# The second sparse tile of an expert layer: half of its value rows weighed and added on VectorE instead of by matmuls

## The chip, the cores and the metric

One core of a Trainium2 chip runs the whole kernel in one launch. The metric is the device time of that launch in microseconds (us), lower is better. TensorE is called PE here, its weight loads PEld, VectorE DVE, ScalarE ACT, GpSimd POOL and SyncE SP.

## The reference, cut to what matters

One layer over 512 latent tokens of width 1024: attention, and then a retrieval of single-neuron experts. The attention part is untouched by the change. The retrieval is this:

```python
def one(xc):                                   # a chunk of 128 tokens
    ...
    ids = ...                                  # (128, 8, 16): 16 experts for each of 8 heads
    g = jax.nn.softmax(best, axis=-1)
    ue = jnp.take(u, ids, axis=0)              # u, v: (16384, 1024) float32
    ve = jnp.take(v, ids, axis=0)
    a = jax.nn.gelu(jnp.einsum('cd,chkd->chk', xc, ue), approximate=False)
    return jnp.einsum('chk,chkd->cd', (g * a).astype(xc.dtype), ve)
```

So each token has 128 slots (8 heads times 16), each slot an expert number and a weight, and a token's output is the sum over its 128 slots of weight times a row of 1024 values of the table v.

## The kernel before, in words

The 512 tokens are four tiles of 128. Tiles 1 and 2 are **dense**: a loop of 128 steps (line 1218) reads the whole tables u and v, 128 rows a step, and works with matmuls whose operands are split in a high and a low part of a narrower float format, so that one product is three matmuls (`mm3`, lines 93 to 96). In each step, and in two halves `b` of it, `split_u` and `split_v` split what was loaded (ACT makes the high part at line 90, DVE the low part at line 91: tiles `uhi`, `ulo`, `vhi`, `vlo`), `scores_u` multiplies tokens with u into `pa`, `weigh` (line 1187) makes the weights from `pa` (gelu on ACT, line 1193; times the gates on DVE, line 1194; high part on ACT, low part on DVE: `ga`, `wdhi`, `wdlo`), and `add_v` adds the weighted rows of v into `accd`.

Tiles 0 and 3 (`FIRST`, `LAST`) are **sparse**: only the rows that a token needs are fetched, by gathers on POOL (`gather`, line 425). One gather brings 128 rows of 4 KB, 512 KB in all, into one of nine buffers that are used in turn (`gbuf`). `sparse_u` takes the 128 slots one by one: a gather brings for each of the 128 tokens its row of u, and one DVE instruction (line 917) multiplies and sums it. `sparse_v` (line 934) then turns weights and expert numbers around by two transposes, so that a gather (`idT`) brings all 128 slots of one token. A group of four gathers, of tokens that lie 32 apart, is used by matmuls (line 957): the weights stand in a masked tile `wm` of 32 columns, of which only that token's is not zero, so the four tokens' matmuls lie in four column strips of PE. After 32 groups `acc` holds the tile's output, and `finish` (line 927) scales it, adds the residual, normalizes and stores.

The gathers are pulled from a generator (`sparse`, line 1167) inside the dense loop, at a pace that spreads what is left evenly over its steps (lines 1243 to 1245). A gather's use is not written at once but put off (`later`, `settle`, lines 876 to 903): a use on DVE until five more gathers have been issued (`LAG2`), a group of four for PE until eight have. The gathers of tile 0's v and tile 3's u are mixed until about 1480 us; from there on all gathers are tile 3's v. Until about 1620 us the dense loop also builds gates for its last quarter (`gates`, lines 1102 to 1113, on DVE, PE and ACT). A scheduler then lays the instructions out engine by engine; each engine runs its own in the order that it has them.

Loads of u and v for the dense loop go through SP's queue (lines 1028 and 1033), 512 KB each, with three buffers for u and two for v.

Of the kernel before, what the change touches and what calls it, by code (L numbers as in the profile page):

```python
# [12 lines left out]
F32 = mybir.dt.float32  # L13
F32R = mybir.dt.float32r
BF16 = mybir.dt.bfloat16
I32 = mybir.dt.int32
U32 = mybir.dt.uint32
AF = mybir.ActivationFunctionType
OP = mybir.AluOpType
# [3 lines left out]
P = 128  # L23
D = 1024
# [14 lines left out]
SLOTS = PH * TOPK  # L39
NEG = -3.0e38  # L40
SB = 16
FIRST, DENSE, LAST = 0, (1, 2), 3
# [19 lines left out]
def tile_layer(ctx: ExitStack, tc: tile.TileContext, aps):  # L62
    nc = tc.nc
# [3 lines left out]
    ident = cst.tile([P, P], F32, name="ident")  # L67
# [64 lines left out]
    for t in range(NKT):  # L132
        xt[t] = xp.tile([P, D], F32, name=f"x{t}")
        src = aps["ctx"][0, t * P : (t + 1) * P, :] if t < NCT else aps["x"][0, (t - NCT) * P : (t - NCT + 1) * P, :]
        (nc.scalar if t % 2 else nc.sync).dma_start(xt[t], src)

    pt = ps0.tile([P, 80], F32, name="pt", tag="t")
# [249 lines left out]
    keep = ctx.enter_context(tc.tile_pool(name="keep", bufs=1, side="right"))  # L387
    rows_ = {}
# [23 lines left out]
    idis = {t: keep.tile([P, SLOTS], I32, name=f"idi{t}") for t in SPARSE}  # L412
    idfs = {t: keep.tile([P, SLOTS], F32, name=f"idf{t}") for t in SPARSE}
    gs = {t: keep.tile([P, TOPK, PH], F32, name=f"g{t}") for t in SPARSE}
    seld = {}
    u_tab = aps["peer_u"][0]
    v_tab = aps["peer_v"][0]
# [3 lines left out]
    def gather(tab, col):  # L421
        pool, tag, n = gbufs["all"][gbufs["n"] % len(gbufs["all"])]
        gbufs["n"] += 1
        b_ = (gp if pool == "gp" else pool).tile([P, D], F32, name="gbuf", tag=tag, bufs=n)
        nc.gpsimd.indirect_dma_start(  # L425
            out=b_, out_offset=None, in_=tab, in_offset=bass.IndirectOffsetOnAxis(ap=col, axis=0)
        )
        return b_
# [141 lines left out]
    def norm_row(pool, src, a_row, dst, add_row=None):  # L570
        s_ = pool.tile([P, 1], F32, name="nss", tag="nss")
        nc.scalar.activation(dst, src, AF.Square, accum_out=s_)
        r_ = pool.tile([P, 1], F32, name="nrs", tag="nrs")
        rsqrt_mean(r_, s_, D)
        nc.vector.scalar_tensor_tensor(dst, src, r_, a_row, op0=OP.mult, op1=OP.mult)
        if add_row is not None:
            nc.vector.tensor_tensor(dst, dst, add_row, op=OP.add)
# [293 lines left out]
    acts = {}  # L871
# [4 lines left out]
    def later(use, several=False):  # L876

        pending.append((gbufs["n"], several, use))
        settle()

    def settle(all_of=None):
        while pending:
            n, several, use = pending[0]
            if all_of is None:
                out = gbufs["n"] - n
                full = out + 1 >= len(gbufs["all"])
                if not several and out < lag[0]:
                    return
                if several and not full and (out < lag[0] + GROUP - 1 or sum(p[1] for p in pending) < GROUP):
                    return  # L890
            elif all_of not in [p[2] for p in pending]:
                return
            if not several:
                pending.pop(0)
                use(0)
                use(1)
                continue
            group = [p for p in pending if p[1]][:GROUP]
            for p in group:
                pending.remove(p)  # L900
            for b in range(2):
                for p in group:
                    p[2](b)

    def flush(use):
        settle(use)

    def sparse_u(t):
        a = gp.tile([P, SLOTS], F32, name="a", tag="a", bufs=2)
        acts[t] = a  # L910
        for k in range(SLOTS):
            ub = gather(u_tab, idis[t][:, k : k + 1])

            def use(b, ub=ub, k=k):
                if b:
                    return
                tc.keep_in_program_order(nc.vector.scalar_tensor_tensor(ub, ub, 1.0, h2s[t], op0=OP.mult, op1=OP.mult, accum_out=a[:, k : k + 1]))  # L917

            later(use)
            yield  # L920
        flush(use)

    def load_x1(t, x1):
        nc.sync.dma_start(x1, out[0, t * P : (t + 1) * P, :])
        return x1

    def finish(t, acc, x1):
        o = gp.tile([P, D], F32, name="o", tag="gbuf", bufs=GBUFS)
        nc.vector.tensor_tensor(o, acc.rearrange("p b n -> p (b n)"), rows_["g2"], op=OP.mult)
        nc.vector.tensor_tensor(x1, x1, o, op=OP.add)  # L930
        norm_row(fp, x1, rows_["fg"], o)
        nc.sync.dma_start(out[0, t * P : (t + 1) * P, :], o)

    def sparse_v(t):
        a = acts[t]
        nc.scalar.activation(a, a, AF.Gelu)
        nc.vector.tensor_tensor(a, a, gs[t].rearrange("p k h -> p (k h)"), op=OP.mult)
        pt = psV.tile([P, 2, 512], F32, name="ptw", tag="acc")
        nc.tensor.transpose(pt[:, 0, :P], a, ident)
        nc.tensor.transpose(pt[:, 1, :P], idfs[t], ident)  # L940
        wT = vp.tile([P, 4, 32], F32, name="wT", tag="wT")
        nc.vector.tensor_copy(wT.rearrange("p c r -> p (c r)"), pt[:, 0, :P])
        idT = vp.tile([P, P], I32, name="idT", tag="idT")
        nc.vector.tensor_copy(idT, pt[:, 1, :P])
        acc = psV.tile([P, 2, 512], F32, name="acc", tag="acc")
        for r in range(32):
            if r % 4 == 0:
                wm = vp.tile([P, 4, 4, 32], F32, name="wm", tag="wm", bufs=2)
                nc.vector.tensor_tensor(
                    wm, eye32[:, r : r + 4].unsqueeze(1).to_broadcast([P, 4, 4, 32]),  # L950
                    wT[:, :, r : r + 4].unsqueeze(3).to_broadcast([P, 4, 4, 32]), op=OP.mult,
                )
            for c in range(4):
                vb = gather(v_tab, idT[:, 32 * c + r : 32 * c + r + 1])

                def use(b, vb=vb, w=wm, c=c, r=r):
                    tc.keep_in_program_order(nc.tensor.matmul(  # L957
                        acc[32 * c : 32 * c + 32, b, :], w[:, c, r % 4], vb[:, 512 * b : 512 * b + 512],
                        start=(r == 0), stop=(r == 31), skip_group_check=True,
                    ))  # L960

                later(use, True)
                yield
        x1 = load_x1(t, keep.tile([P, D], F32, name="x1f", tag="a2"))
        flush(use)
        while "fg" not in rows_:
            yield
        finish(t, acc, x1)

    gp = ctx.enter_context(tc.tile_pool(name="gp", bufs=1, side="right"))  # L970
    slx = ExitStack()
    sl = slx.enter_context(tc.tile_pool(name="sl", bufs=2, side="right"))
    o = [gp.tile([P, KC, P], F32, name="o0", tag="gbuf", bufs=GBUFS)]
# [9 lines left out]
    def early():  # L983
        for _ in first:
            posts[0] += 1
            yield
        posts[0] = NK
        g2 = mod_rows(pp0, psP, "a", ("g2",))
        for k, _ in enumerate(sparse_u(FIRST)):
            if k in (6, 12, 18):  # L990
                next(g2, None)
            yield
        gbufs["all"].append(("gp", "h2x", 1))
        lag[0] = max(lag[0], LAG1)
        yield from sparse_v(FIRST)
# [3 lines left out]
    o = [gp.tile([P, KC, P], F32, name="oT", tag="ox", bufs=3) for _ in rest]  # L999
# [7 lines left out]
    vp = ctx.enter_context(tc.tile_pool(name="vp", bufs=1, side="right", reuse_waits="tile"))  # L1007
    eye32 = vp.tile([P, 32, 32], BF16, name="eye32")
# [5 lines left out]
    psV = ctx.enter_context(tc.tile_pool(name="psV", bufs=1, space=PSUM, reuse_waits="tile"))  # L1014
# [101 lines left out]
    with ExitStack() as es:  # L1116
# [36 lines left out]
        n = NPRE // 2  # L1153
# [13 lines left out]
    def sparse():  # L1167

        second, n, share = sparse_u(LAST), 0, 0.95 * (2 * SLOTS - gbufs["n"]) / SLOTS
        for _ in second:  # L1170
            yield
            n += share
            while n >= 1:
                n -= 1
                if next(fill, fill) is not fill:
                    yield
        for _ in fill:
            yield
        yield from sparse_v(LAST)

    psB = ctx.enter_context(tc.tile_pool(name="psB", bufs=1, space=PSUM, reuse_waits="tile"))
    psD = ctx.enter_context(tc.tile_pool(name="psD", bufs=1, space=PSUM, reuse_waits="tile"))
    sp = sparse()
    fd = ctx.enter_context(tc.tile_pool(name="fd", bufs=2, reuse_waits="tile"))
    accd = psD.tile([P, len(DENSE), 2, 512], F32, name="accd")

    def weigh(i):
# [30 lines left out]
    for i in range(NK + 2):  # L1218
        q, e = i // QI, i % QI
# [32 lines left out]
    for s in range(len(DENSE)):  # L1252
        finish(DENSE[s], accd[:, s], x1d[s])
# [50 lines left out]
```

## Time and profile before

| | |
|---|---|
| median of 3 runs (lowest, highest) | 1859.14 us (1855.89, 1860.36) |
| the profiled execution: its time / its span | 1860.77 us / 1859.0 us |
| mean granted clock of PE | 0.937 |
| busy: PE, DVE, ACT, POOL | 86%, 70%, 39%, 37% |
| read from memory | 472.88 MB, 257 GB/s over the span |

PE's busy time counts matmuls that overlap, so a busy PE is not PE at its peak. A share over the whole span is a mean of stages with different limits; stages are read in the windows below.

### The profile page before, as it was taken

How to read it: one execution, taken by the hardware profiler on the slowest of the kernel's cores; microseconds unless marked ns; L12 is line 12 of the kernel's file. 1: busy time of each engine (PE TensorE's matmuls, PEld its weight loads, DVE VectorE, ACT ScalarE, POOL GpSimd, SP SyncE). 2: the span in 40 equal slices, each digit the busy share in tenths (PEclk: the TensorE clock that was granted, in tenths of full speed). 3: DMA queues.
4: the chain of work that ended last, by engine and by line, in shares of the span. 5: the costliest groups of instructions: out<-in, count | busy, mean ns of one | idle time of the engine just before them, and what ended most of it. 6: DMA issues, size and time to landing. Idle time of an engine off the chain costs nothing.

```text
span 1859.0 us, 30825 instructions
## 1 busy us (share of the span) xinstructions
PE 1592.6 (86%) x11767; PEld 1225.0 (66%) x11767; DVE 1293.1 (70%) x2923; ACT 732.8 (39%) x1441; POOL 693.0 (37%) x607
## 2 busy tenths in 40 slices
PE   4999898757788577898499899899999989999996
PEld 1778567636563476566266778787778767777774
DVE  3623534687776898998688789798889855555545
ACT  4432554435661232111144444344444433444443
POOL 2212200045554685443424334344344333343431
PEclk9999988976889799999799999899999999999998
DMA  8222633555559885967577898898899798899994
GB/s 298 76 68 68 230 97 122 187 186 172 185 189 324 289 315 217 381 242 255 190 271 261 303 333 301 294 354 303 321 344 354 263 362 280 298 347 357 352 353 168
DMA packets 148085, 479.10 MB, mean 258 GB/s; under 512 B 15889, under 2 KB 16993, under 8 KB 147937
## 3 DMA queue, kind: packets, MB, share of 16 engines
q0 software_dynamic: 73728, 268.47, 40.7%
q1 hardware_dynamic: 73200, 206.96, 31.3%
q8 instruction: 92, 1.51, 0.3%
q10 hardware_dynamic: 1008, 1.70, 0.3%
q14 instruction: 57, 0.46, 0.1%
HBM read 472.88 MB, written 4.19 MB: 257 GB/s over the span
## 4 chain that ended last, share of the span: by engine, by line
PE 37%; DVE 5%; DMA 4%; issue 4%; ACT 1%; POOL 1%; another core or an unknown queue 0%; ACTq 0%; DVEq 0%; POOLq 0%; SPq 0%
PE accd L94 6%; PE accd L96 5%; PE acc L957 5%; PE accd L95 5%; PE pa L94 5%; PE pa L96 5%; PE pa L95 4%; PE pg L1111 3%; DMA vraw<-in_peer_v_dram 2%; DMA gbuf<-in_peer_u_dram,idi 1%; DVE gbuf L917 1%; DVE vlo L91 1%; POOL gbuf L425 1%; DMA gbuf<-in_peer_v_dram,idT 1%; DVE oj L1102 1%
## 5 line engine op out<-in xcount | busy, mean ns | idle before, releaser
L425 POOL DMA_INDIRECT gbuf<-in_peer_v_dram,idT x256 | 275.4, 1076 | 457.6 <-PE acc L957 290.5
L425 POOL DMA_INDIRECT gbuf<-in_peer_u_dram,idi x256 | 314.8, 1230 | 312.1 <-DVE gbuf L917 169.4
L917 DVE SCALAR_TENSOR_TENSOR gbuf<-gbuf,h 128x1024 f32<-128x1024 f32 x256 | 320.7, 1277 | 32.1 <-DMA gbuf<-in_peer_u_dram,idi 31.6
L90 ACT CAST vhi<-vraw 128x512 fp32r<-128x512 f32 x256 | 157.8, 620 | 254.0 <-PE accd L96 196.2
L91 DVE TENSOR_TENSOR vlo<-vraw,vhi 128x512 fp32r<-128x512 f32 x256 | 174.9, 688 | 115.5 <-ACT vhi L90 88.2
L94 PE MATMUL pa<-h2Thi,uhi 128*128 128x256 f32 x848 | 244.6, 288 | 11.1 <-ACT ga L1193 10.2
L95 PE MATMUL pa<-h2Tlo,uhi 128*128 128x256 f32 x848 | 242.9, 286 | 0.6 <-issue 0.6
L96 PE MATMUL pa<-h2Thi,ulo 128*128 128x256 f32 x848 | 242.5, 286 | 0.8 <-issue 0.8
L94 PE MATMUL accd<-vhi,wdhi 128*128 128x512 f32 x512 | 215.4, 421 | 21.1 <-ACT wdhi L90 17.2
L96 PE MATMUL accd<-vhi,wdlo 128*128 128x512 f32 x512 | 207.0, 404 | 6.0 <-DVE wdlo L91 4.8
L95 PE MATMUL accd<-vlo,wdhi 128*128 128x512 f32 x512 | 206.7, 404 | 3.5 <-DVE vlo L91 2.7
L91 DVE TENSOR_TENSOR ulo<-uraw,uhi 128x512 fp32r<-128x512 f32 x212 | 146.6, 692 | 57.7 <-ACT uhi L90 47.8
L90 ACT CAST uhi<-uraw 128x512 fp32r<-128x512 f32 x212 | 131.3, 620 | 129.3 <-PE pa L95 65.4
L94 PEld LDWEIGHTS pa<-h2Thi,uhi 128*128 128x128 f32 x848 | 165.0, 195 | 26.1 <-ACT ga L1193 16.3
L95 PEld LDWEIGHTS pa<-h2Tlo,uhi 128*128 128x128 f32 x848 | 164.9, 194 | 9.1 <-issue 1.1
L96 PEld LDWEIGHTS pa<-h2Thi,ulo 128*128 128x128 f32 x848 | 164.6, 194 | 2.1 <-issue 1.6
L94 PEld LDWEIGHTS accd<-vhi,wdhi 128*128 128x128 f32 x512 | 98.6, 193 | 76.7 <-issue 38.9
L957 PE MATMUL acc<-gbuf,wm 128*32 128x512 f32 x1024 | 143.7, 618 | 0.9 <-DMA gbuf<-in_peer_v_dram,idT 0.6
L1102 DVE TENSOR_TENSOR oj<-iota,ijT 128x2048 bf16<-128x2048 bf16 x64 | 79.9, 1248 | 76.8 <-PE accd L96 24.2
L1111 PE MATMUL pg<-og,oj 128*128 128x32 bf16 x3072 | 101.0, 177 | 34.8 <-DVE og L1107 20.0
L1111 PEld LDWEIGHTS <-oj 128*128 128x128 bf16 x3072 | 88.2, 97 | 56.4 <-issue 26.7
L96 PEld LDWEIGHTS accd<-vhi,wdlo 128*128 128x128 f32 x512 | 98.0, 192 | 34.7 <-DVE wdlo L91 12.2
(278 smaller groups left out, 2855.3 us busy)
## 6 DMA issues: line engine op xcount, KB each, us to landing
uraw<-in_u_turned_dram SPq DMA_DIRECT2D x128, 512.0 KB
vraw<-in_peer_v_dram SPq DMA_DIRECT2D x128, 512.0 KB
wraw<-in_w_mod_dram SPq DMA_DIRECT2D x24, 1024.0 KB
wraw<-in_peer_wq_dram SPq DMA_DIRECT2D x16, 1024.0 KB
wraw<-in_w_in_dram SPq DMA_DIRECT2D x8, 1024.0 KB
wraw<-in_w_out_dram SPq DMA_DIRECT2D x4, 1024.0 KB
wraw<-in_w_out_dram SPq DMA_DIRECT2D x8, 512.0 KB
gbuf<-in_peer_u_dram,idi POOLq DMA_INDIRECT x256
```

The lines of the kernel that those rows point to most:

```text
L90: nc.scalar.copy(hi, src)
L91: (eng or nc.vector).tensor_tensor(lo, src, hi.bitcast(F32), op=OP.subtract)
L94: nc.tensor.matmul(ps, ahi, bhi, start=first, stop=False)
L95: nc.tensor.matmul(ps, ahi, blo, start=False, stop=False)
L96: nc.tensor.matmul(ps, alo, bhi, start=False, stop=last)
L425: nc.gpsimd.indirect_dma_start(out=b_, out_offset=None, in_=tab, in_offset=bass.IndirectOffsetOnAxis(ap=col, axis=0))
L917: tc.keep_in_program_order(nc.vector.scalar_tensor_tensor(ub, ub, 1.0, h2s[t], op0=OP.mult, op1=OP.mult, accum_out=a[:, k : k + 1]))
L957: tc.keep_in_program_order(nc.tensor.matmul(acc[32 * c : 32 * c + 32, b, :], w[:, c, r % 4], vb[:, 512 * b : 512 * b + 512], start=(r == 0 ...
L1102: nc.vector.tensor_tensor(oj, row(iota2, NK), over(ijT[t][:, 1, ts], NK), op=OP.is_equal)
L1111: nc.tensor.matmul(pg[:, r], oj[:, r // 2, :, r % 2], og[:, w, r // 2, :, r % 2], start=(w == 0), stop=(w == 2))
```

## The change

The second sparse tile (tile 3) gets `sparse_v_halves` in place of `sparse_v`; tile 0 keeps `sparse_v`. Of the 128 slots, the last 64 are still used by matmuls, but a gather now brings two tokens with 64 slots each, so that the 128 tokens take 64 gathers and 16 groups of four. The first 64 slots are gathered slot by slot, as for u: a gather brings for each of the 128 tokens its row of v for one slot, and one DVE instruction multiplies it with the token's weight and adds it to the tile `sums` in SBUF (4 KB in each partition, new). Four gathers of the one kind and four of the other alternate, 128 in all as before. `finish` adds `sums` and `acc` by one more DVE instruction. The tile of masked weights is built in two halves of 64 partitions, and the two transposes read a copy (`twice`) in which the 64 slots stand twice.

```diff
-    def finish(t, acc, x1):
+    def finish(t, acc, x1, more=None):
...
-        nc.vector.tensor_tensor(o, acc.rearrange("p b n -> p (b n)"), rows_["g2"], op=OP.mult)
+        if more is None:
+            nc.vector.tensor_tensor(o, acc.rearrange("p b n -> p (b n)"), rows_["g2"], op=OP.mult)
+        else:
+            nc.vector.tensor_tensor(more, more, acc.rearrange("p b n -> p (b n)"), op=OP.add)
+            nc.vector.tensor_tensor(o, more, rows_["g2"], op=OP.mult)
...
+    HS = SLOTS // 2
+    def sparse_v_halves(t, sums):
...
+        for w, src in enumerate((a, idfs[t])):
+            nc.vector.tensor_copy(tw[:, w], src[:, HS:].unsqueeze(1).to_broadcast([P, 2, HS]))
...
+        for r in range(16):
+            if r % 4 == 0:
+                wm = vp.tile([P, 4, 4, 32], F32, name="wm", tag="wm", bufs=2)
+                for e in range(2):
...
+            for c in range(4):
+                vb = gather(v_tab, idT[:, 16 * c + r : 16 * c + r + 1])
+
+                def use(b, vb=vb, w=wm, c=c, r=r):
+                    tc.keep_in_program_order(nc.tensor.matmul(
+                        acc[32 * c : 32 * c + 32, b, :], w[:, c, r % 4], vb[:, 512 * b : 512 * b + 512],
+                        start=(r == 0), stop=(r == 15), skip_group_check=True,
+                    ))
+
+                later(use, True)
+                yield
+            for k in range(4 * r, 4 * r + 4):
+                vb = gather(v_tab, idis[t][:, k : k + 1])
+
+                def add(b, vb=vb, k=k):
...
+                    if k == 0:
+                        ins = nc.vector.tensor_scalar(sums, vb, a[:, 0:1], None, op0=OP.mult)
+                    else:
+                        ins = nc.vector.scalar_tensor_tensor(sums, vb, a[:, k : k + 1], sums, op0=OP.mult, op1=OP.add)
...
+                later(add)
+                yield
...
-        yield from sparse_v(LAST)
+        yield from sparse_v_halves(LAST, sums)
...
+    sums = ctx.enter_context(tc.tile_pool(name="sums", bufs=1)).tile([P, D], F32, name="sums")
```

On DVE, late in the dense loop (no gates are built there any more), one step and a half stood like this before; `ulo` and `vlo` are the low parts of the loads, `ga` and `wdlo` those of the weights:

```order
L1194 TENSOR_TENSOR ga<-ga,Gb 128x256
L91 TENSOR_TENSOR vlo<-vraw,vhi 128x512
L91 TENSOR_TENSOR wdlo<-ga,wdhi 128x256
L91 TENSOR_TENSOR ulo<-uraw,uhi 128x512
L91 TENSOR_TENSOR vlo<-vraw,vhi 128x512
L91 TENSOR_TENSOR ulo<-uraw,uhi 128x512
L1194 TENSOR_TENSOR ga<-ga,Gb 128x256
```

Now a like place reads as follows (line 1194 is now 1262, and line 1028 is the new addition):

```order
L91 TENSOR_TENSOR wdlo<-ga,wdhi 128x256
L1028 SCALAR_TENSOR_TENSOR sums<-gbuf,a,sums 128x1024
L91 TENSOR_TENSOR ulo<-uraw,uhi 128x512
L1028 SCALAR_TENSOR_TENSOR sums<-gbuf,a,sums 128x1024
L91 TENSOR_TENSOR vlo<-vraw,vhi 128x512
L1028 SCALAR_TENSOR_TENSOR sums<-gbuf,a,sums 128x1024
L1262 TENSOR_TENSOR ga<-ga,Gb 128x256
L91 TENSOR_TENSOR ulo<-uraw,uhi 128x512
```

Three of a block's four additions stand in one step, one of them directly ahead of `ga`; the fourth comes a step later, and a third step has none.

On POOL, the order of the gathers from where tile 3's u ends was this before:

```order
L425 DMA gbuf<-in_peer_u_dram,idi_1502 128x1024 x2
L425 DMA gbuf<-in_peer_v_dram,idT 128x1024 x2
L425 DMA gbuf<-in_peer_u_dram,idi_1502 128x1024 x4
L425 DMA gbuf<-in_peer_v_dram,idT 128x1024 x132
L1299 UNCONDITIONAL_BRANCH
```

Now the gathers for PE (`idT`) and for DVE (`idi`) alternate by fours from the same place on:

```order
L425 DMA gbuf<-in_peer_u_dram,idi_1502 128x1024 x4
L425 DMA gbuf<-in_peer_v_dram,idT 128x1024 x8
L425 DMA gbuf<-in_peer_v_dram,idi_1502 128x1024 x4
L425 DMA gbuf<-in_peer_v_dram,idT 128x1024 x4
L425 DMA gbuf<-in_peer_v_dram,idi_1502 128x1024 x4
```

Their number is the same; which engine gives a buffer back is what differs.

At the end of the kernel DVE's order now is this, where before `o<-acc` came directly behind the last `wdlo`:

```order
L1028 SCALAR_TENSOR_TENSOR sums<-gbuf,a,sums 128x1024
L91 TENSOR_TENSOR wdlo<-ga,wdhi 128x256
L1028 SCALAR_TENSOR_TENSOR sums<-gbuf,a,sums 128x1024 x2
L932 TENSOR_TENSOR sums<-sums,acc 128x1024
L933 TENSOR_TENSOR o<-sums,g_3192 128x1024
```

The last additions and one more instruction of 128x1024 stand ahead of the tile's scaling.

## Rows read from the trace of the kernel before

**Rows 1.** The page: engines over the span, and the span in 40 slices.
```profile
PE 1592.6 (86%) x11767; PEld 1225.0 (66%) x11767; DVE 1293.1 (70%) x2923; ACT 732.8 (39%) x1441; POOL 693.0 (37%) x607
...
PE   4999898757788577898499899899999989999996
DVE  3623534687776898998688789798889855555545
...
DMA  8222633555559885967577898898899798899994
```

**Rows 2.** Windows: stretch, PE, PEld, DVE, ACT, POOL busy, clock, DMA share, GB/s.
```profile
1050.00:1450.00 400.00, 376.06 (x3270) 311.24 (x3269) 342.08 (x636) 171.68 (x333) 164.54 (x141) 0.97 0.89 323
1500.00:1620.00 120.00, 113.07 (x1015) 86.87 (x1014) 65.56 (x120) 47.73 (x93) 40.47 (x42) 1.00 0.86 303
1640.00:1800.00 160.00, 160.00 (x1063) 120.96 (x1061) 80.34 (x139) 70.03 (x135) 61.66 (x62) 1.00 0.95 357
```

**Rows 3.** The chain of waits, late: start us, length us, what.
```profile
1644.34 1.85 PE acc L957 x16
...
1818.91 1.85 PE acc L957 x16
1839.73 3.62 PE acc L957 x32
```

**Rows 4.** Groups by line, 1640 to 1800 us: busy, mean ns, idle before.
```profile
L425 POOL DMA_INDIRECT gbuf<-in_peer_v_dram,idT x62 | 62.4, 1006 | 98.6 <-PE acc L957 84.6 <-issue 11.9 <-PE accd L96 1.2
...
L957 PE MATMUL acc<-gbuf,wm 128*32 128x512 f32 x256 | 30.8, 598 | 0.0
```

**Rows 5.** Windows, as in rows 2: the fullest stretches of the DMA engines.
```profile
740.00:790.00 50.00, 41.53 (x208) 26.42 (x207) 44.55 (x246) 6.64 (x14) 23.63 (x23) 0.92 0.99 379
750.00:760.00 10.00, 10.00 (x48) 5.91 (x42) 8.10 (x57) 0.00 (x0) 7.02 (x8) 0.93 1.02 409
1690.00:1700.00 10.00, 10.00 (x68) 7.54 (x68) 4.96 (x10) 4.71 (x9) 3.63 (x4) 1.00 1.00 358
```

**Rows 6.** Groups by line, 1050 to 1450 us (u gathered slot by slot).
```profile
L917 DVE SCALAR_TENSOR_TENSOR gbuf<-gbuf,h 128x1024 f32<-128x1024 f32 x99 | 119.2, 1220 | 6.9 <-DMA gbuf<-in_peer_u_dram,idi 6.9
L94 PE MATMUL pa<-h2Thi,uhi 128*128 128x256 f32 x409 | 118.4, 289 | 6.6 <-ACT ga L1193 6.0 <-issue 0.5
...
L94 PE MATMUL accd<-vhi,wdhi 128*128 128x512 f32 x205 | 86.8, 424 | 5.0 <-ACT wdhi L90 4.5 <-issue 0.4
```

**Rows 7.** Timeline of PE: the same place in two halves of a dense step.
```profile
1659.60 0.40 PE L94 MATMUL accd<-vhi,wdhi 128*128 128x512 f32 x1
...
1662.42 0.40 PE L94 MATMUL accd<-vhi,wdhi 128*128 128x512 f32 x1
```

**Rows 8.** Timeline, all engines: from scores to weights in one dense step.
```profile
1823.50 0.28 PE L96 MATMUL pa<-h2Thi,ulo 128*128 128x256 f32 x1
...
1825.02 0.42 DVE L1194 TENSOR_TENSOR ga<-ga,Gb 128x256 f32<-128x256 f32 x1
...
1826.47 0.42 DVE L91 TENSOR_TENSOR wdlo<-ga,wdhi 128x256 fp32r<-128x256 f32 x1
...
1826.94 0.19 PEld L96 LDWEIGHTS accd<-vhi,wdlo 128*128 128x128 f32 x1 [0.30 <-DVE wdlo L91]
```

**Rows 9.** Timeline of DVE at the end.
```profile
1843.37 1.23 DVE L929 TENSOR_TENSOR o<-acc,g 128x1024 f32<-128x1024 f32 x1 [6.25 <-PE acc L957]
1844.51 1.22 DVE L929 TENSOR_TENSOR o<-accd,g 128x1024 f32<-128x1024 f32 x1
```

**Rows 10.** Timeline of PE after a stall, and the window around it (columns of rows 2).
```profile
1493.31 0.79 PE L94 MATMUL accd<-vhi,wdhi 128*128 128x512 f32 x1 [3.55 <-ACT wdhi L90]
...
1490.00:1500.00 10.00, 6.69 (x24) 5.89 (x25) 4.90 (x9) 3.71 (x8) 3.02 (x3) 0.66 1.02 382
```

More of the change, by code (lines that the diff above doesn't have):

```diff
@@ L968, in sparse_v @@
         finish(t, acc, x1)
+    HS = SLOTS // 2
+    def sparse_v_halves(t, sums):
+        a = acts[t]
+        nc.scalar.activation(a, a, AF.Gelu)
+        nc.vector.tensor_tensor(a, a, gs[t].rearrange("p k h -> p (k h)"), op=OP.mult)
+        twice = vp.tile([P, 4, 4, 32], F32, name="twice", tag="wm", bufs=2)
+        tw = twice.rearrange("p a b c -> p (a b c)").rearrange("p (w d k) -> p w d k", w=4, k=HS)
+        for w, src in enumerate((a, idfs[t])):
+            nc.vector.tensor_copy(tw[:, w], src[:, HS:].unsqueeze(1).to_broadcast([P, 2, HS]))
+        pt = psV.tile([P, 2, 512], F32, name="ptw", tag="acc")
+        for w in range(2):
+            nc.tensor.transpose(pt[:, w, :P], tw[:, w].rearrange("p d k -> p (d k)"), ident)
+        wT = vp.tile([P, 4, 32], F32, name="wT", tag="wT")
+        idT = vp.tile([P, P], I32, name="idT", tag="idT")
+        eye = eye32.rearrange("p (r e) n -> p r e n", e=2)
+        for e in range(2):
+            hs = slice(64 * e, 64 * e + 64)
+            for dst, w in ((wT.rearrange("p c r -> p (c r)"), 0), (idT, 1)):
+                nc.vector.tensor_copy(dst[hs, 0:64], pt[hs, w, :P].rearrange("p (r e) -> p r e", e=2)[:, :, e])
+        wv = wT.rearrange("p c r -> p (c r)")[:, 0:64].rearrange("p (c r) -> p c r", c=4)
+        acc = psV.tile([P, 2, 512], F32, name="acc", tag="acc")
+        for r in range(16):
+            if r % 4 == 0:
+                wm = vp.tile([P, 4, 4, 32], F32, name="wm", tag="wm", bufs=2)
+                for e in range(2):
+                    hs = slice(64 * e, 64 * e + 64)
+                    nc.vector.tensor_tensor(
+                        wm[hs], eye[hs, r : r + 4, e].unsqueeze(1).to_broadcast([64, 4, 4, 32]),
+                        wv[hs, :, r : r + 4].unsqueeze(3).to_broadcast([64, 4, 4, 32]), op=OP.mult,
+                    )
+            for c in range(4):
[10 more added lines that the diff above has]
+                def add(b, vb=vb, k=k):
+                    if b:
+                        return
+                    if k == 0:
+                        ins = nc.vector.tensor_scalar(sums, vb, a[:, 0:1], None, op0=OP.mult)
+                    else:
+                        ins = nc.vector.scalar_tensor_tensor(sums, vb, a[:, k : k + 1], sums, op0=OP.mult, op1=OP.add)
+                    tc.keep_in_program_order(ins)
+                later(add)
+                yield
+        x1 = load_x1(t, keep.tile([P, D], F32, name="x1f", tag="a2"))
+        flush(add)
+        finish(t, acc, x1, sums)
```

## The prediction

> **What bounds the kernel now.** I read the page first, then windows, then the chain of waits, then groups and timelines in the stretch that the change touches. The page's slices say where to look [rows 1]: in the last quarter PE stands at 8 or 9 tenths in every slice but the last, DVE falls to 5 tenths, and the DMA engines stand at 7 to 9. The means over the span (PE 86%, DVE 70%) don't show this. The windows show it by stage [rows 2]. From 1640 to 1800 us PE is busy 160 of 160 us at full clock, DVE 80.3 us (50%), and the DMA engines 0.95 at 357 GB/s. From 1500 to 1620 us, where gates are still built, PE is idle 6.9 us of 120, and the DMA engines have more room (0.86). The chain agrees: it runs through PE, and the groups of line 957 stand on it at 1.85 us each [rows 3]. Between the first and the last row there lie 17 such steps, (1818.91 - 1644.34) / 17 = 10.27 us from group to group. POOL, which issues the gathers, is idle 98.6 of these 160 us and waits mostly for those matmuls to give buffers back [rows 4]; it bounds nothing. So PE bounds the end of the kernel, and the DMA engines are 5% behind it.
>
> The change replaces two groups (eight gathers) by one group and four additions on DVE. I call eight gathers a block: before, 2 x 10.27 = 20.54 us, in which 357 GB/s move 7.33 MB.
>
> **The change, part by part.**
>
> *Matmuls removed.* 32 groups become 16. Each costs 1.85 us on PE [rows 3], also where it is waited for last: 16 x 1.85 = 29.6 us off. The last row shows two groups back to back at the end (3.62 us); one of them goes, and is counted here.
>
> *Additions added.* 64 instructions of 128x1024 on DVE. The trace doesn't show this form; the nearest row is line 917, one instruction over as many elements with one sum per token, 1220 ns, and instructions of that size follow each other 1.14 us apart [rows 6, 9]. So 64 x 1.14 = 73 us of DVE, 4.6 us a block. DVE's share late goes from 50% to about (10.3 + 4.6) / 19.6 = 76%, less than the 342 of 400 us that it works from 1050 to 1450 us [rows 2]. DVE has the time; the question is whom an addition delays. The tight place is the way from scores to weights [rows 8]: the scores are done at 1823.8, DVE's `ga` starts at 1825.02, its `wdlo` at 1826.47, and the weight load that takes it has already waited 0.3 us at 1826.94. An addition that stands in front of either is paid by PE. In the new order 19 of the 64 stand directly ahead of one of the two. And a step with three additions gives DVE about 6.6 us of work (four low parts at 0.61, two at 0.35, three at 1.14) while PE needs 2 x 2.82 = 5.64 us [rows 7]. The bounds: nothing (the stretch from 1050 to 1450 us with 99 such instructions has PE idle 6.0%, that from 1500 to 1620 us without them 5.8% [rows 2]), and 19 x 1.14 = 21.7 us. I take what PE waited for that way in the stretch with 99 of them, 6.0 + 4.5 = 10.5 us [rows 6], 0.11 us each: 0.44 us a block, 7 us in all.
>
> *A new wait on DVE.* An addition waits for its gather, with `ulo`, `vlo`, `ga` and `wdlo` queued behind it and PE waiting for those. I cost it at nothing: line 917 has the same lag of five gathers and the same nine buffers, and its 99 instructions waited 6.9 us for gathers in 400 us [rows 6]. If that cover goes, it is the rival below.
>
> *The DMA engines.* The gathers, their bytes and the loads are the same; only their time gets shorter. For PE alone a block would take 20.54 - 1.85 = 18.69 us, with DVE's delays 19.13 us; that needs 7.33 MB / 19.13 us = 383 GB/s. What can they move? From below, 358 GB/s at a share of 1.00 for 10 us; from above 409 GB/s for 10 us, and 379 for 50 us at 0.99 [rows 5]. I take 357 / 0.955 = 374 GB/s, this stretch's own mix without the idle 4.5% (the window's share is 0.95 to two places), which lies near the 50 us row. A block then takes 7.33 / 0.374 = 19.60 us, 0.94 us less than now.
>
> *The sum.* In PE's new order 5 of the 16 groups stand where gates are built and 11 behind. There the engines have room: 5 x (1.85 - 0.44) = 7.1 us. Behind: 11 x 0.94 = 10.3 us. At the very end one more DVE instruction stands between the last matmul and the output: +1.1 us [rows 9]. The rest I cost at nothing: two copies into `twice`, four small copies in place of two and eight half-tiles of `wm` in place of eight whole ones are about 1 us of DVE once, while tile 3's last u rows are worked off; PE has dense steps to do then. POOL issues as many gathers as before, SP's loads keep their number and swap places with each other at a few points, which can hardly be worth more than their half step. Together -16.3 us: 1860.8 - 16.3 = 1844.5 us for the profiled execution. That lies 1.6 us over the median, so 1843 for the median.
>
> **A rule against this change.** From 740 to 790 us the DMA engines move 379 GB/s, more than late [rows 5]; whether they can in the late mix is open. In the Trainium skill the page "DMA: Bandwidth & Descriptors" (section "Where 436 GB/s comes from") says that for traffic between HBM and SBUF the HBM side binds at about 358 GB/s per core. By that the stretch is full already, and the sum would be the third rival's 1854. The trace differs by its 379 and 409.
>
> **The rivals.**
>
> 1. *PE alone decides.* The DMA engines follow to 392 GB/s, as they did from 750 to 760 us, and DVE delays nobody. -29.6 + 1.1: 1831 us for the median. For it: DVE's low share. Against: 392 GB/s would have to hold for 200 us.
>
> 2. *Slower: DVE holds PE up.* Late in the kernel the queues are fuller than from 1050 to 1450 us (0.95 against 0.89), gathers land later, and the first addition of each four waits at the head of DVE. What a long wait costs is seen at 1493 us: PE waited 3.55 us for `wdhi`, and in the 10 us around it the granted clock is 0.66 instead of 1.0, part of the time at 1.2 GHz instead of 2.4 [rows 10]. That is 3.55 us, and up to 10 x 0.34 = 3.4 us of clock behind it, some 6 us in all. The gain goes when a block loses 28.5 / 16 = 1.8 us against PE's own sum. With one such event in every second block, 8 x 6 = 48: 1859 - 28.5 + 48 = 1879 us. Against it: the 6.9 us of rows 6.
>
> 3. *The DMA engines are full at 358.* Then a block behind the gates takes 20.5 us as now, and only the 5 blocks with gates gain: -7.1 + 1.1 = -6, less a little: 1854 us for the median. For it: the row at 1690 us, share 1.00 at 358 GB/s [rows 5].
>
> 4. *Nothing comes of it.* The blocks with gates lose on DVE, which builds the gates there, what they gain on PE, and the others stay at 20.5 us: 1859 us.
>
> **How the numbers follow.** My forecast gets 0.45 (1838 to 1850), rival 1 0.15, rival 2 0.12, rival 3 0.20, rival 4 0.08. A measurement of this kernel can tell about 0.3%, 5.6 us, from no change. Faster by more, under 1853.5: forecast, rival 1 and half of rival 3, 0.70. Within: the other half and most of rival 4, 0.17. Slower by more: rival 2 and a rest, 0.13. The range goes from rival 1 to just past no change, 1830 to 1860; it leaves out rival 2 and the far edge of rival 1. The additions at 21.7 us instead of 7 would give about 1852, still inside.
>
> **What would show it.** Right: 16 groups on PE, one about every 19.6 us late; DMA share 0.98 or more and 370 to 380 GB/s; DVE near 75%; PE no longer at 160 of 160 but some 95%; few waits of line 1028 for gathers. Rival 1 shows PE still full and 390 GB/s; rival 2 long waits of line 1028 for DMA and a granted clock under 1.0 behind 1640 us; rival 3 357 GB/s and blocks of 20.5 us. My forecast is wrong if the blocks with gates gain nothing, or if the late blocks gain more than 1.5 us each.

## The result, and the profile after

| | before | changed |
|---|---|---|
| median (lowest, highest), runs side by side | 1859.75 us (1855.89, 1862.97) | 1835.37 us (1830.04, 1837.89) |
| ratio, 95% interval | | 0.986 (0.9832 to 0.9888) |
| profiled execution: time / span | 1860.77 / 1859.0 us | 1837.89 / 1836.1 us |

The change is 24.4 us faster (by the interval, 21 to 31 us). The forecast was 16 us faster. Two more comparisons gave 0.9876 (0.9849 to 0.9904) and 0.9839 (0.9785 to 0.9892), told below.

The page of the changed kernel, lines that answer to [rows 1]: engines over the span, and the 40 slices.

```profile
PE 1561.8 (85%) x11511; PEld 1216.0 (66%) x11511; DVE 1361.3 (74%) x2992; ACT 731.4 (40%) x1441; POOL 715.2 (39%) x607
...
PE   4999888856778477889769989999999999999995
...
DVE  2633544587875898899488968898888987787876
...
DMA  7222534456559886877767778899988989999994
```

DVE gained 68 us of work, and in the last eight slices it stands at 6 to 8 tenths where it stood at 4 or 5 [rows 1]. PE stands at 9 in every slice of the last quarter but the last one, much as before.

The windows of the changed kernel, in the columns of [rows 2] (PE, PEld, DVE, ACT, POOL busy, clock, DMA share, GB/s):

```profile
1500.00:1620.00 120.00, 112.85 (x987) 91.63 (x985) 92.94 (x151) 51.62 (x101) 54.55 (x43) 0.99 0.93 338
1620.00:1780.00 160.00, 159.98 (x1033) 131.64 (x1030) 124.08 (x186) 76.36 (x149) 79.53 (x71) 1.00 1.00 391
1640.00:1800.00 160.00, 159.46 (x1028) 130.89 (x1027) 122.78 (x183) 75.78 (x147) 78.46 (x71) 1.00 1.01 393
```

From 1620 to 1780 us PE is idle 0.02 us in 160, DVE is at 124.08 / 160 = 78%, and the DMA engines went from 0.95 at 357 GB/s to 1.00 at 391 to 393. PE did not become the engine with room that the forecast made it (95%). It still sets the pace, and the DMA engines followed it.

The chain of waits of the changed kernel, which answers to [rows 3] (start us, length us, what):

```profile
1618.41 1.85 PE acc L1012 x16
...
1785.57 1.85 PE acc L1012 x16
1817.21 1.98 PE acc L1012 x16
1819.21 1.23 DVE sums L932
1820.47 1.22 DVE o L933
```

Between the first two rows lie nine blocks: (1785.57 - 1618.41) / 9 = 18.57 us for a block of eight gathers, against 20.54 before, a gain of 1.97 us each. PE's own sum in the prediction was 18.69. The last two rows are the end: the new instruction on DVE (line 932) stands between the last group and the scaling.

Groups by line of the changed kernel, 1620 to 1780 us (busy, mean ns of one, idle before and its cause):

```profile
L1028 DVE SCALAR_TENSOR_TENSOR sums<-gbuf,a,sums 128x1024 f32<-128x1024 f32 x35 | 44.8, 1279 | 1.2 <-DMA gbuf<-in_peer_v_dram,idi 1.2
...
L1012 PE MATMUL acc<-gbuf,wm 128*32 128x512 f32 x132 | 16.0, 598 | 0.0
```

35 additions waited 1.2 us in all for their gathers. An addition lasts 1279 ns, where line 917 took 1220 [rows 6], and with nothing to wait for the next instruction starts 1.20 us after it (1.14 in the forecast).

**Where the time went.** DVE's multiplication with the gates (`ga`, line 1194 before, 1262 now) comes once in each of the last 106 of the 128 dense steps (the first 22 make their weights another way). I count them from 0 and use them as marks (the runs' expectations call them steps). Up to mark 57 (about 1470 us) both kernels run the same instructions. Timeline of DVE, marks 57, 75 and 103, of the kernel before:

```profile
1470.69 0.43 DVE L1194 TENSOR_TENSOR ga<-ga,Ga 128x256 f32<-128x256 f32 x1 [0.47 <-ACT ga L1193]
...
1624.34 0.42 DVE L1194 TENSOR_TENSOR ga<-ga,Gb 128x256 f32<-128x256 f32 x1
...
1825.02 0.42 DVE L1194 TENSOR_TENSOR ga<-ga,Gb 128x256 f32<-128x256 f32 x1
```

and of the changed kernel:

```profile
1477.89 0.43 DVE L1262 TENSOR_TENSOR ga<-ga,Ga 128x256 f32<-128x256 f32 x1 [0.45 <-ACT ga L1261]
...
1619.83 0.42 DVE L1262 TENSOR_TENSOR ga<-ga,Gb 128x256 f32<-128x256 f32 x1
...
1801.02 0.43 DVE L1262 TENSOR_TENSOR ga<-ga,Gb 128x256 f32<-128x256 f32 x1
```

| us | before | changed | difference |
|---|---|---|---|
| start to mark 57 (unchanged part) | 1470.7 | 1477.9 | +7.2 |
| 57 to 75 (gates are built) | 153.7 | 141.9 | -11.7 |
| 75 to 103 (no gates) | 200.7 | 181.2 | -19.5 |
| 103 to the end | 34.0 | 35.1 | +1.1 |

So the part that was changed gained 31 us in this pair. 7 us of it was given back ahead of the change, where nothing was changed: single executions of one program differ there by that much, as the experiments show.

### The profile page after: what moved, and what is told of

The parts are those of the page before. It is cut to its first block, busy times and chain, and to the rows that moved or that the text cites. A ratio compares the mean times of both kernels' runs of the same rounds, so it can differ in the third digit from the quotient of the medians.

```text
span 1836.1 us, 30378 instructions
## 1 busy us (share of the span) xinstructions
PE 1561.8 (85%) x11511; PEld 1216.0 (66%) x11511; DVE 1361.3 (74%) x2992; ACT 731.4 (40%) x1441; POOL 715.2 (39%) x607
## 4 chain that ended last, share of the span: by engine, by line
PE 52%; DVE 21%; DMA 10%; issue 7%; ACT 5%; POOL 3%; another core or an unknown queue 1%; ACTq 0%; SPq 0%; POOLq 0%; DVEq 0%
PE accd L94 5%; PE accd L96 5%; PE accd L95 5%; PE pa L94 4%; PE pa L96 4%; PE pa L95 4%; DVE gbuf L917 4%; DMA vraw<-in_peer_v_dram 3%; PE pg L1178 3%; DMA gbuf<-in_peer_u_dram,idi 3%; DMA wraw<-in_peer_wq_dram 2%; POOL gbuf L425 2%; PE S L485 2%; PE pp L95 2%; PE acc L961 2%
## 5 line engine op out<-in xcount | busy, mean ns | idle before, releaser
L425 POOL DMA_INDIRECT gbuf<-in_peer_u_dram,idi x256 | 313.5, 1225 | 314.5 <-DVE gbuf L917 168.3
L425 POOL DMA_INDIRECT gbuf<-in_peer_v_dram,idT x192 | 222.9, 1161 | 306.7 <-PE acc L961 114.2
L95 PEld LDWEIGHTS accd<-vlo,wdhi 128*128 128x128 f32 x512 | 98.3, 192 | 23.8 <-DVE vlo L91 7.3
```

The lines of the kernel that those rows point to most:

```text
L95: nc.tensor.matmul(ps, ahi, blo, start=False, stop=False)
L425: nc.gpsimd.indirect_dma_start(out=b_, out_offset=None, in_=tab, in_offset=bass.IndirectOffsetOnAxis(ap=col, axis=0))
```

## The experiments

Three theories stood against each other. **Theory 1:** PE alone decides late; additions and gathers lie beside it (rival 1). **Theory 2:** the DMA engines are full late, at what they then move. **Theory 3:** the additions hold PE up, 0.11 us each, as the sum had it. In the table, late is 1620 to 1780 us (for e1 to e4, whose chip is faster, 1580 to 1700), and the marks are those above.

| run | ratio (95%) | 57 to 75 | 75 to 103 | late PE / DVE / DMA share, GB/s |
|---|---|---|---|---|
| e1_again | 0.9876 (0.9849 to 0.9904) | 135.2 | 179.9 | 100% / 76% / 1.01, 394 |
| e2_no_adds | 1.0128 (1.0102 to 1.0153) | 153.0 | 216.3 | 91% / 44% / 0.89, 325 |
| e3_no_gathers | 0.9821 (0.9789 to 0.9852) | 129.7 | 179.9 | 100% / 78% / 0.79, 268 |
| e4_three_quarters | 1.0044 (1.0021 to 1.0068) | 147.4 | 199.0 | 90% / 81% / 0.97, 365 |
| e5_before_again | 1.0017 (0.9992 to 1.0042) | 151.6 | 200.1 | 100% / 51% / 0.94, 353 |
| e6_short_adds | 0.9905 (0.9879 to 0.9931) | 142.4 | 190.8 | 96% / 56% / 0.97, 371 |
| e7_adds_twice | 1.0122 (1.0095 to 1.0149) | 149.2 | 220.2 | 89% / 85% / 0.89, 330 |
| e8_three_quarters_no_gathers | 0.9784 (0.9747 to 0.9822) | 136.4 | 176.6 | 98% / 89% / 0.62, 204 |
| e9_short_same_order | 0.9863 (0.9807 to 0.9919) | 142.0 | 185.4 | 98% / 56% / 1.00, 388 |
| e10_short_groups | 0.9753 (0.9699 to 0.9807) | 138.7 | 176.4 | 96% / 78% / 1.00, 396 |
| e11_changed_again | 0.9839 (0.9785 to 0.9892) | 144.2 | 181.9 | 100% / 78% / 1.00, 393 |

Runs e1 to e4 share a chip, e5 to e8 another, e9 to e11 a third; the medians of the kernel before there were 1802.43, 1853.55 and 1857.67 us. A ratio always stands against the kernel before on the same chip.

**e1_again: the changed kernel once more.** No edit.

> The changed kernel itself, timed again, to tell how much of its gain is the change and how much differs from one execution to the next. PE decides: 16 groups less at 1.85 us and one more DVE instruction at the end, 28.5 us off, 1831 us. The DMA engines decide at 374 GB/s, as forecast: 1843 us. Measured so far: 1835 us, 24.4 us off. I expect 1833 to 1837 us.

1779.07 us on a chip where the kernel before takes 1802.43: the absolute time was missed, since this chip is faster, the ratio was not. PE was busy 120.00 of 120 us late, with the DMA engines at 394 GB/s.

**e2_no_adds: 63 additions left out.**

```diff
-                    if b:
+                    if b or k:
                         return
```

> The changed kernel with 63 of its 64 additions left out (the gathers stay; so that half of the slots is missing from tile 3's output). If additions delay PE by 0.11 us each, as forecast, this is 7 us faster than the changed kernel: 1828 us. If PE bounds the end and DVE's additions lie beside it: 1834 to 1836 us, at most 1.5 us faster. If the DMA engines bound the end: no change either, 1835 us.

A miss in every theory: 48 us slower than the changed kernel beside it (1827.26 against 1779.07). Waits of this run, 1580 to 1700 us (engine, line, waited for: us, times, longest):

```profile
POOL gbuf L425 <- DMA gbuf<-in_peer_v_dram,idi: 55.9, 17, 8.9
...
PEld acc L1012 <- DMA gbuf<-in_peer_v_dram,idT: 17.6, 7, 3.5
```

A gather whose rows nobody reads holds its buffer until it has landed itself. In this run such a buffer comes round again early, though there are nine; two rows of POOL's timeline that follow each other:

```profile
1616.55 0.97 POOL L425 DMA_INDIRECT gbuf<-in_peer_v_dram,idi  x1 [0.30 <-issue]
1624.62 0.95 POOL L425 DMA_INDIRECT gbuf<-in_peer_v_dram,idT  x1 [7.10 <-DMA gbuf<-in_peer_v_dram,idi]
```

POOL issues in order, so it stood 55.9 of 120 us waiting for landings, later gathers were issued late, and PE's groups then waited for theirs. The orders of PE and SP moved as well, exactly as in e6 below. The edit took an addition away and put a worse wait in its place; it says nothing about the additions. In the changed kernel POOL waits too, 59.6 of 160 us for the additions (`POOL gbuf L425 <- DVE sums L1028`), but PE's groups find their rows there.

**e3_no_gathers: the additions' 64 gathers left out.**

```diff
-                vb = gather(v_tab, idis[t][:, k : k + 1])
+                vb = rows_["g2"]
+                gbufs["n"] += 1
```

> The changed kernel with the 64 gathers of the additions left out; each addition reads a tile that lies in SBUF already (so that half of the slots of tile 3's output is made from the wrong rows). The bytes of eight slots fall from 7.3 to 5.2 MB. If the DMA engines bound the end (share 1.00, 391 GB/s), this is faster by more than 5 us: under 1830 us. If PE bounds it: 1832 to 1836 us, with PE still busy 160 of 160 us late and a DMA share near 0.75.

PE's, ACT's and SP's orders are the changed kernel's, row for row. Late window of this run, and below it that of e1:

```profile
1580.00:1700.00 120.00, 120.00 (x780) 97.67 (x778) 94.12 (x142) 57.66 (x112) 22.00 (x22) 1.00 0.79 268
```

```profile
1580.00:1700.00 120.00, 120.00 (x774) 98.69 (x771) 91.64 (x139) 57.06 (x112) 59.51 (x53) 1.00 1.01 394
```

A third less traffic, and marks 75 to 103 take 179.9 us in both. Late it is PE that sets the pace of the changed kernel. The whole run is 8.5 us shorter in the median, though, which the expectation had kept for full DMA engines, and that has to come from elsewhere: in the profiles 5.5 us of it lie between marks 57 and 75, where gates are built and PE has gaps, and 3.3 us ahead of mark 57.

**e4_three_quarters: 96 slots on DVE, 32 by matmuls.** Eight groups, four tokens of 32 slots in each of their gathers, twelve additions to every four such gathers.

```diff
-    HS = SLOTS // 2
+    NM = 32
+    E = P // NM
+    HS = SLOTS - NM
...
-        for r in range(16):
+        R = NM // 4
+        for r in range(R):
...
-            for k in range(4 * r, 4 * r + 4):
+            for k in range(HS // R * r, HS // R * r + HS // R):
```

> 96 of the 128 slots gathered slot by slot and added on DVE, 32 by matmuls, four tokens per gather: 8 groups on PE instead of 16. If only PE decides: 8 x 1.85 = 14.8 us faster than the changed kernel, 1820 us, and the DMA engines would have to move 413 GB/s late. If they are full at 391 to 400 GB/s: 1830 to 1837 us, with PE no longer busy all the time. If additions delay PE by 0.11 us each: 3.5 us less gain than by PE alone, 1824 us.

A miss: 31 us slower than the changed kernel, and slower than the kernel before. Rows of the chain of waits (start us, length us, what), and below them the waits from 1580 to 1700 us:

```profile
1607.09 0.70 DVE vlo L91
1607.80 8.07 DMA vraw<-in_peer_v_dram
...
1655.59 0.61 DVE vlo L91
1656.22 7.85 DMA vraw<-in_peer_v_dram
```

```profile
POOL gbuf L425 <- DVE sums L1031: 52.4, 34, 6.3
...
ACT vhi L90 <- DMA vraw<-in_peer_v_dram: 19.0, 9, 3.5
PEld accd L94 <- ACT wdhi L90: 10.8, 6, 3.6
```

The chain now runs through loads of v that land late, ACT waits 19.0 us for them, and PE for ACT. Each of these loads starts as soon as DVE's `vlo` is done, which gives one of the two buffers of v back; so a `vlo` that stands behind additions also delays the next load. DVE at 81%, the DMA engines or both together could be the cause; e8 takes the transfers away.

**e5_before_again: the kernel before, for its profile.** No edit.

> The kernel before once more, for its profile on the same chip as the runs beside it. All theories: no change against the kernel before (ratio 1.00), steps 57 to 103 of the dense loop in 345 to 355 us, a block of eight gathers late in about 20.5 us, PE full late at 0.95 of the DMA engines and 357 GB/s. If the late block were already near 20.0 us on this chip, part of what the changed kernel shows would be the chip and not the change.

As expected. With e11, which ran on another chip (medians of the kernel before 1853.55 and 1857.67 us), it gives a second pair: 57 to 75 went from 151.6 to 144.2 us (-7.4), 75 to 103 from 200.1 to 181.9 (-18.2), 103 to the end from 34.1 to 35.0.

**e6_short_adds: each addition cut to 32 columns.**

```diff
-                        ins = nc.vector.scalar_tensor_tensor(sums, vb, a[:, k : k + 1], sums, op0=OP.mult, op1=OP.add)
+                        ins = nc.vector.scalar_tensor_tensor(sums[:, 0:32], vb[:, 0:32], a[:, k : k + 1], sums[:, 0:32], op0=OP.mult, op1=OP.add)
```

> The changed kernel with each of the 64 additions cut to 32 of its 1024 columns, so that the output is not the whole sum: the waits, the order, the gathers and the buffers that the additions give back stay, only DVE's time of some 1.15 us each goes to about 0.1 us. Prices the additions on PE. Theory 1 (PE decides late and the additions lie beside it): within 0.3% of the changed kernel, ratio to the kernel before 0.985 to 0.990, late block 18.5 us. Theory 2 (the DMA engines are full): the same, no gain. Theory 3 (each addition costs PE 0.11 us as in the prediction): 7 us less than the changed kernel, ratio about 0.983, and shorter waits of PE for wdhi and wdlo in steps 57 to 75.

None of the three: with 35 us less DVE work in 160 (89.67 against 124.43 in e11) it is no faster than the changed kernel, and in its profile it is slower, PE idle 6.3 us late. The edit did more than it says. The scheduler lays the instructions out by its own durations, and with a shorter addition it moved rows. At five places PE's order changed like this: three matmuls of the scores (`pa`) went behind the products (`accd`) that they had been mixed with (`-` marks their old places):

```
 L96 MATMUL pa<-h2Thi,ulo 128x256
-L94 MATMUL pa<-h2Thi,uhi 128x256
-L95 MATMUL pa<-h2Tlo,uhi 128x256
 L94 MATMUL accd<-vhi,wdhi 128x512
 L95 MATMUL accd<-vlo,wdhi 128x512
-L96 MATMUL pa<-h2Thi,ulo 128x256
 L96 MATMUL accd<-vhi,wdlo 128x512
```

Rows of the other engines moved as well. e9 takes that out.

**e7_adds_twice: each addition issued twice.**

```diff
                     tc.keep_in_program_order(ins)
+                    tc.keep_in_program_order(nc.vector.scalar_tensor_tensor(sums, vb, a[:, k : k + 1], sums, op0=OP.mult, op1=OP.add))
```

> The changed kernel with each addition issued twice, so that the added rows count double in the output. DVE's work in a late block goes from some 14.2 to 18.8 us, beside 18.6 us of PE. Theory 1 (DVE lies beside PE as long as it has room): the room is used up, DVE becomes the bound or close to it, late block 19 to 20 us, 10 to 30 us more than the changed kernel, ratio 0.993 to 1.003. Theory 3 (each addition costs PE 0.11 us): 7 us more, ratio about 0.991. Theory 2 (the DMA engines are full): a gather's buffer comes back later, which only a slower block shows; no more than 5 us.

The direction is theory 1's, and the size is beyond it: ratio 1.0122 against 0.993 to 1.003. DVE is busy 135.94 of 160 us late (85%), not full, and the loads of v land late as in e4 (ACT waits 23.9 us for them). Here too the scheduler moved rows, some 260 lines of difference on PE against 30 in e6, so the run shows neither what an addition costs nor at what share DVE's room ends: e8, below, has DVE busier with PE hardly idle.

**e8_three_quarters_no_gathers: e4 without its 96 gathers for additions.** The edit is that of e3, made to e4; PE's, ACT's and SP's orders are e4's, row for row.

> The version with 96 slots on DVE and 32 by matmuls, with the 96 gathers of the additions left out; the additions read a resident tile instead, so that the output is not the reference's. DVE, PE and ACT do all that they did there, the DMA engines move 50 MB less. If the DMA engines (loads of v that land late) are what made that version slow: PE full late, some 8 x 1.85 = 15 us less than the changed kernel, ratio about 0.975. If DVE is: PE still waits for wdhi and wdlo as there, ratio 0.995 to 1.005.

From 1.0044 to 0.9784 (0.9747 to 0.9822), near the 0.975 expected if transfers are the cause. Late window of this run:

```profile
1620.00:1780.00 160.00, 156.98 (x994) 132.28 (x993) 142.41 (x205) 78.27 (x153) 10.94 (x11) 1.00 0.62 204
```

DVE's order is e4's too, it does all of its additions and is busy 89%, and PE is idle only 3.0 us in 160. So DVE's work alone did not stop e4; it took the transfers of the gathers beside it. The rows of e4 show how the two can meet: a load asked for late, behind additions, that then takes 8 us to land (median of all loads of v late: 7.5 us in e4, 6.5 in e1, 4.8 in e3, on one chip). How much of e4's loss is the late asking and how much the slow landing was not separated, nor was the order of the gathers, twelve in a row for the additions instead of four.

**e9_short_same_order: the short additions of e6, in the changed kernel's order.** The 63 instructions are replaced after scheduling by the same ones with 32 columns; no engine's order differs from the changed kernel's.

```diff
+def columns(p):
+    if len(p.ap) != 2 or list(p.ap[1]) != [1, D]:
+        return p
+    return mybir.PhysicalAccessPattern(
+        ap=[list(p.ap[0]), [1, 32]], offset=p.offset, dtype=p.dtype, memref=p.memref, memsetref=p.memsetref
+    )
...
+    for block in nc.main_func.blocks:
+        if any(i.name in ADDS for i in block.instructions):
+            block.instructions = [resized(i) if i.name in ADDS else i for i in block.instructions]
```

> The changed kernel with 63 of its 64 additions cut to 32 of 1024 columns, as in the run of short additions before it, so that the output is not the whole sum, but cut only after the scheduler has laid out the instructions: every engine's order is the changed kernel's, row for row. In the earlier run the scheduler had moved rows of PE, ACT, DVE, SP and POOL, so its lost time may be the order's. Theory 1 (the additions lie beside PE, the earlier loss was the order): within 0.3% of the changed kernel beside it, ratio 0.984 to 0.990, late block 18.5 us, PE full late. Theory 3 (each addition costs PE 0.11 us): 7 us less than the changed kernel, ratio about 0.983. A third reading (gathers given back earlier crowd the loads of v, whatever the order): 10 us more than the changed kernel, as in the earlier run, late block 19 to 20 us, PE waiting for loads of v.

1834.95 us beside e11's 1831.43: not faster, where theory 3 wanted 7 us less. (The ratio's interval alone would hold theory 3's 0.983; run beside run on one chip decides it: the fastest of e9's five runs, 1832.21 us, lies above e11's median.) Late windows, e9 and below it e11:

```profile
1620.00:1780.00 160.00, 156.56 (x1013) 128.74 (x1012) 90.29 (x183) 75.52 (x147) 67.41 (x68) 1.00 1.00 388
```

```profile
1620.00:1780.00 160.00, 159.98 (x1034) 130.56 (x1034) 124.43 (x186) 76.53 (x150) 75.60 (x68) 1.00 1.00 393
```

DVE's late share fell from 78% to 56% and nothing came of it. Late, the additions cost PE nothing in this order; theory 3 falls. The expectation's third reading falls too: ACT waited only 2.3 us for loads of v. The profile has PE idle 3.4 us late, waiting for the gelu on ACT, which e11 has not; with five runs each, 3.5 us between the medians is too little to read. That e6's loss came from its order is what e6 and e9 together suggest (0.9905 and 0.9863, intervals that overlap), not more.

**e10_short_groups: 14 of the 16 groups cut to 32 columns, in the same order.** The same replacement, made to the matmuls of line 1012.

> The changed kernel with the matmuls of 14 of tile 3's 16 groups cut to 32 of 512 columns after the scheduler has laid out the order, so that the output is not the whole sum; orders, waits, gathers and loads stay. PE's sum for a late block falls from 18.6 to about 17.2 us, for which the DMA engines would have to move 7.33 MB / 17.2 us = 426 GB/s. If 391 to 394 GB/s is all that the DMA engines can do (theory 2: PE and the DMA engines end together in the changed kernel): late block 18.6 us as there, PE idle some 8% late, ratio as the changed kernel. If they were only following PE: late block 17.2 to 17.8 us, over 400 GB/s, 10 to 20 us less than the changed kernel, ratio about 0.98.

Groups by line, 1620 to 1780 us, and the window:

```profile
L1029 PE MATMUL acc<-gbuf,wm 128*32 128x32 f32 x144 | 3.0, 201 | 0.0
```

```profile
1620.00:1780.00 160.00, 153.41 (x1057) 133.65 (x1056) 124.41 (x188) 77.62 (x153) 80.56 (x71) 0.98 1.00 396
```

A group now takes 0.26 us on the chain in place of 1.85, and PE's sum for a late block is 18.57 - 1.59 = 17.0 us. Yet 75 to 103 takes 176.4 us, 3% less than e11's 181.9, where PE's sum fell by 8.6%. PE is idle 6.6 us in 160 and its clock 0.98, with long steps of the chain on transfers (lines renumbered by the edit's helpers):

```profile
1640.24 12.15 DMA gbuf<-in_peer_v_dram,idi
...
1778.65 0.70 DVE vlo L108
1779.38 8.27 DMA vraw<-in_peer_v_dram
...
1792.39 0.61 DVE vlo L108
1793.02 6.56 DMA vraw<-in_peer_v_dram
```

So the transfers, theory 2, come in right behind PE: the DMA engines gave 396 GB/s at a share of 1.00 where PE's sum alone would have asked for 7.33 MB / 17.0 us = 431. By this run PE is last in the changed kernel by about 3%. What then takes over isn't bandwidth alone, since here too the loads of v are asked for when DVE's `vlo` is done; the two were not separated. The whole run is 13 us below e11; the profiles put 5.4 us of it between marks 75 and 103 and 5.5 between 57 and 75.

**e11_changed_again: the changed kernel beside e9 and e10.** No edit.

> The changed kernel, unchanged, beside the two runs before it on the same chip. All theories: ratio 0.984 to 0.990, late block 18.5 us, PE full late, the DMA engines at a share of 1.00 and 391 to 394 GB/s.

1831.43 us; the ratio's 0.9839 lies just under the 0.984 to 0.990 that was expected. The late window has PE at 159.98 of 160 and 393 GB/s, as in the first trace.

## Why the prediction was right on the sign and short on the size

The sign, the range and the work moved were right; the time came out 8 us under the forecast, between it and rival 1's 1831. That it lay inside the range says little for the mechanism, as the range began just below rival 1's time. By the prediction's own signs its account of the late part was wrong, and rival 1's, which had got 0.15, was what happened there. Point by point:

- **Matmuls removed, 1.85 us each: right.** A group still takes 1.85 us on the chain, and the stretch between marks 57 and 103 got shorter by 31.2 us in one pair and 25.6 in the other, around the 29.6 of the sum.
- **Additions, 0.11 us of PE each: wrong, late they cost nothing measurable.** The step took all of PE's waits for `ga` and `wdhi` in the stretch of u as the price of line 917's instructions [rows 6]. Late, PE idled 0.02 us in 160 beside 35 additions, and e9 shows that cutting them short brings nothing. Whom those waits in the earlier stretch belong to was not tried. Where gates are built, e9 was 2.2 us shorter than e11 (142.0 against 144.2), which is what the sum takes there (5 x 0.44) but less than single profiles differ by. DVE's share fits (76% forecast, 78% measured) partly by luck: its work in a block is 124.08 x 18.57 / 160 = 14.4 us and not 14.9, in a shorter block.
- **The wait of additions for gathers, nothing: right,** 1.2 us in 160.
- **The DMA ceiling of 374 GB/s: the step that failed.** "357 / 0.955 = 374" read a share of 0.95 as if the engines' busy time were work that can't be done faster. The same transfers, asked for sooner, ran at 391 to 394 GB/s for 120 to 160 us at a share of 1.00 (e1, e11, the first trace), and at 396 when PE left more room (e10). That lies nearer the forecast's upper bound, 409 GB/s, than its lower, 358 [rows 5]. So a late block gained 1.97 us and not 0.94; by the marks the late part gained 19.5 and 18.2 us where 10.3 was forecast. The prediction's own sign of being wrong, late blocks that gain more than 1.5 us each, came true.
- **Blocks with gates, 7.1 us: right in size.** 11.7 and 7.4 us were measured between marks 57 and 75; the first pair had the kernel before stall for 3.55 us in it [rows 10]. That this part is a mixture shows in e3: without the additions' traffic it would be 5.5 us shorter still.
- **The tail, +1.1 us: right,** +1.1 and +0.9.
- **Rivals.** Late, rival 1 happened to the letter: PE full, 391 to 394 GB/s, blocks of 18.57 us against its 18.69. The third, full at 358 GB/s, did not: with one core running, the changed kernel held 391 to 394. The Trainium skill's page "DMA: Bandwidth & Descriptors" (section "Where 436 GB/s comes from") says that for traffic between HBM and SBUF the HBM side binds at about 358 GB/s per core; no run here shows that limit, and e10 moved 396. Rival 2's mechanism, additions that wait for their gathers, did not appear (1.2 us in 160), not even in e4 and e7, where they waited 0.0 us late; only e10 had 6.4 us of it. What it named as the consequence, PE waiting for `wdhi`, did appear there (9.6 us of 120 in e4, 14.8 of 160 in e7), behind late loads of v: the changed kernel stops short of that.

Why the measured 24 us lies under rival 1's 28.5 is only partly shown. The changed part gained 31 and 26 us in two pairs of profiles; how far the unchanged part adds or takes 5 to 7 us for some other reason than chance is open.

## What to carry to other kernels

A share of busy DMA engines and the GB/s beside it need not be a ceiling: here 0.95 at 357 GB/s became 1.00 at 391 when the same transfers were asked for sooner. Look for the fullest stretch of any length in the same trace, and give the ceiling the range between. When work moves from the engine that bounds to one with room, first ask whether the moved instructions stand in the bound engine's path at all: beside a full PE, 35 additions at 78% of DVE cost nothing, while one step more of the same (e4) turned into late loads and lost everything. There, ask also what gives a load its buffer: here DVE's `vlo`, which stood behind the additions. And an edit made ahead of a scheduler can change its order too, as e2, e6 and e7 did; compare orders before reading an experiment, or edit behind it.

## What the runs showed of the hardware that was not expected

- Gathers with no reader held POOL's queue for 55.9 of 120 us: their buffers came back only with their own landing, and the next gather was soon waiting for one, 7.10 us in the row shown (e2).
- Loads of v of one size took 4.8, 6.5 and 7.5 us to land (medians late in e3, e1 and e4, one chip), at 268, 394 and 365 GB/s in all.
- The DMA engines held 391 to 394 GB/s in a mix of loads and gathered 4 KB rows for 120 to 160 us, and 396 under more demand.
- The same program took 1802 us on the chip of e1 to e4 and 1854 to 1860 in the other comparisons. Most of it lies ahead of mark 57 (1425.5 us in e1, 1466.4 in e11); what differs between the chips wasn't tried.
- Leaving that chip aside, mark 57 came between 1459.9 and 1477.9 us (both ends without any edit ahead of it in the program). One pair of profiles can't show a difference of 10 us in the whole; stretches between marks can.
